# Row sums from the addition and squares on ScalarE at the feed-forward norms, with the next weights' first high parts emitted earlier

## The chip, the cores and the metric

The kernel runs on one core of a Trainium2 chip. Its time is the device time of one execution in microseconds, and each figure is a median over repeated runs on the same chip. A core has five engines that work side by side, each with its own queue, which it works off in order: TensorE (PE in the profile, with its weight loads as PEld) multiplies matrices, VectorE (DVE) and ScalarE (ACT) work on rows of 128 partitions, GpSimd (POOL) does a little setup, and SyncE (SP) issues most of the transfers from memory. Engines wait for each other by semaphores.

## The reference

Two layers over 256 tokens of width 1024, in float32. Each layer is a half-step feed-forward block, a mixer and another half-step feed-forward block, each followed by a layer norm over the residual:

```python
for l in range(DEPTH):
    h = _swiglu(x, ffn_w1[l, 0], ffn_w3[l, 0], ffn_w2[l, 0])
    x = _layernorm(ALPHA * x + 0.5 * h, ln_g[l, 0], ln_b[l, 0])
    h = _mixer(x, l, ...)
    x = _layernorm(ALPHA * x + h, ln_g[l, 1], ln_b[l, 1])
    h = _swiglu(x, ffn_w1[l, 1], ffn_w3[l, 1], ffn_w2[l, 1])
    x = _layernorm(ALPHA * x + 0.5 * h, ln_g[l, 2], ln_b[l, 2])

def _swiglu(x, w1, w3, w2):
    return (jax.nn.silu(x @ w1) * (x @ w3)) @ w2

def _layernorm(x, g, b):
    mu = jnp.mean(x, axis=-1, keepdims=True)
    var = jnp.mean(jnp.square(x - mu), axis=-1, keepdims=True)
    return (x - mu) * lax.rsqrt(var + LN_EPS) * g + b
```

The mixer (a gated spatial unit, differential attention, gates and an output projection) is not touched by the change.

## The kernel before

The 256 tokens are two tiles of 128 (`t` = 0, 1), the width is two halves of 512 (`c`, or `h`). Every weight comes from memory as a raw block of 128 x 2048 numbers (`raw_pool`, four buffers). `stream` (L154) loads it and splits it: ScalarE copies it to a reduced-precision high part (L173, `whi`), and VectorE subtracts that from the raw block for the low part (L177, `wlo`). A product is the sum of three: high by high, low by high, high by low (`three`, L217). The pools for high and low parts hold eight pieces each.

TensorE's order is written out by hand. The other engines' orders come from a planner at compile time: each instruction has a priority, its place in the program (`step` raises it by 1000 for every block), and goes into its engine's queue when the planner reckons its inputs ready, lower numbers first. `soon` lowers the number by two blocks; `behind(x)` orders an instruction behind x on the same engine. The queues are then worked off as they stand.

`ffn` (L569) ends with the products by the second weight. Four pairs of row blocks are held back (`HELD`): their weights are split early, all eight pieces of the pools, and their products come last, in the order tile 0 half 0, tile 0 half 1, tile 1 half 0, tile 1 half 1, each 24 products of one bank. After each bank the sum goes to the residual `x_tok` and to the norm:

- `Norm.part` (L485) adds the bank to the residual (L490) and takes VectorE's statistics of the 512 columns (bn_stats, L495). It is ordered behind the x split of tile 0, half 0, once there is one.
- `Norm.finish` (L499) joins the statistics (bn_aggr, L502), computes the inverse root on VectorE (`rsqrt`, L185: `ve`, a start value, three rounds of two operations, L189 to L195) and normalises both halves (L506); `ends[t]` is the last of these.
- `Norm.more` (L478) adds other contributions of tile 1 to the residual (L481, L483), behind `ends[0]`.
- `Norm.turned` and `turn` (L546) follow as a side task, at set places in TensorE's order: TensorE transposes a normalised half (L550), ScalarE applies gain and bias (L556, `xf`) and makes x's high part (L182), VectorE its low part (L183). `xlo[t, h]` is that last one.

The next layer begins with `gemm_b2` (L323), two sources of two blocks each. Its first block, and the first half of its second, are split into slots lent from the pool of activations (`lhi`, `llo`), because the pools are full of held pieces; the second half of the second block and the two later blocks go to the pools as the held products free them (`whi`, `wlo`, here 512 wide). Two ordering cells serve this: `early[0]` is the last lent high part, and later high parts go behind it; `after` puts low parts behind `ends[0]` (second and third block) or behind `xlo[0, 1]` (fourth). `gemm_b2` multiplies tile 0 with half 0 of x by blocks one and two (24 products), then half 1 by blocks three and four; tile 1's transposes come after 30 and 42 of these products.

There are three feed-forward norms with a layer behind them, two norms behind mixers, and the last norm, which ends the kernel (`last`) and has its own way through `finish`.

Of the kernel before, what the change touches and what calls it, by code (L numbers as in the profile page):

```python
# [20 lines left out]
P = 128  # L21
# [36 lines left out]
def trunk(ctx, tc, x, xT, w13a, w13b, w2s, w2p, wb, wqk, wa, wbr, wo, gateb, sgug, sgub, sguwT, sgubias, lam, diffg,  # L58
# [18 lines left out]
    def name(s):  # L77
        serial[0] += 1
        return f"{s}_{serial[0]}"
# [24 lines left out]
    def s512(s, n=4):  # L104
        return tmp.tile([P, 512], F32, tag="side", name=name(s), bufs=n)
# [6 lines left out]
    def step():  # L112
        chunk[0] += 1
        tc.cur_priority = chunk[0] * STEP

    tc.cur_priority = 0
    @contextmanager
    def soon():
        was = tc.cur_priority
        tc.cur_priority = max(0, was - 2 * STEP)  # L120
        yield
        tc.cur_priority = was
# [27 lines left out]
    def behind(ins):  # L150

        return tc.issue_after(ins) if ins is not None else nullcontext()

    def stream(src, width=CH, sub=HC, lent=(), after=(None, None)):  # L154

        step()
        raw = raw_pool.tile([P, CH], F32, tag="raw", name=name("raw"))
        nc.sync.dma_start(raw[:, :width], src)  # L160
        out = []
        for o in range(0, width, HC):
            if o // HC in lent:
                hi, lo = ([act.tile([P, 512], F32R, tag="slot", name=name(n)) for _ in range(2)] for n in ("lhi", "llo"))
                at = [(hi[j], lo[j]) for j in range(2)]
            else:
                hi = hi_pool.tile([P, HC], F32R, tag="hi", name=name("whi"))
                lo = lo_pool.tile([P, HC], F32R, tag="lo", name=name("wlo"))
                at = [(hi[:, p : p + sub], lo[:, p : p + sub]) for p in range(0, HC, sub)]
            for p, (h, w) in zip(range(0, HC, sub), at):  # L170
                r = raw[:, o + p : o + p + sub]
                with behind(latest[0] if o // HC in lent else early[0] or latest[0]):
                    copied = A.activation(h, r, AF.Copy)  # L173
                if o // HC in lent:
                    early[0] = copied.ins
                with behind(after[o // HC] or latest[1]):
                    V.tensor_tensor(out=w, in0=r, in1=h.bitcast(F32), op=ALU.subtract)  # L177
            out.append((hi, lo))
        return out

    def split(hi, lo, src):
        a = A.activation(hi, src, AF.Copy)  # L182
        return a.ins, V.tensor_tensor(out=lo, in0=src, in1=hi.bitcast(F32), op=ALU.subtract).ins  # L183

    def rsqrt(v, eps):  # L185


        ve, y = sm("ve", 1), sm("yi", 1, I32)
        V.tensor_scalar(out=ve, in0=v, scalar1=eps, scalar2=None, op0=ALU.add)  # L189
        V.tensor_scalar(out=y, in0=ve.bitcast(I32), scalar1=-0.5, scalar2=RSQRT_START, op0=ALU.mult, op1=ALU.add)  # L190
        y = y.bitcast(F32)
        for e in (-26 / 27, -8 / 9, -2 / 3):
            a, z = sm("nwa", 1), sm("nwy", 1)
            V.tensor_scalar(out=a, in0=y, scalar1=y, scalar2=ve, op0=ALU.mult, op1=ALU.mult)
            V.tensor_scalar(out=z, in0=a, scalar1=3.0 * 2.0 ** e, scalar2=y, op0=ALU.subtract, op1=ALU.mult)  # L195
            y = z
        return y
# [125 lines left out]
    def gemm_b2(srcs, xh, xl, done, norm=None):  # L323

        lent, after = [()] * 4, [(None, None)] * 4
        if norm:
            lent = [(0, 1), (0,), (), ()]
            after[1:3] = [(norm.ends[0], norm.ends[0])] * 2  # L330
        ps = [[bank() for _ in range(2)] for _ in range(NT)]
        got = [[None] * 4 for _ in range(2)]
        for t in range(NT):
            for c in range(2):
                if norm:
                    norm.ready(t, c)
                    after[3] = [norm.xlo.get((0, 1))] * 2
                for m in range(2):
                    n = 2 * c + m
                    if t == 0:  # L340
                        got[m][2 * c : 2 * c + 2] = stream(srcs[m][:, c * CH : (c + 1) * CH], sub=512, lent=lent[n],
                                                           after=after[n])
                    for i in range(2 * c, 2 * c + 2):
                        rows_b(ps[t][m], t, 2 * i, got[m][i], xh, xl, KT)
            early[0] = None
            with behind(latest[0] if t == 0 else None):
                done(t, ps[t])
# [104 lines left out]
    class Norm:  # L452
# [5 lines left out]

        def __init__(self, l, i, scale, eps, after, last=False):
            self.scale, self.eps, self.last, self.done = scale, eps, last, set()  # L460
            self.ends, self.xlo = [None] * NT, {}
            self.gT, self.bT = (v[:, l, i] for v in (ln_g, ln_b))
            self.y = x_tok
            self.group = 256 if last else 512
            self.st = [sm("st", D // self.group * 6, bufs=2) for _ in range(NT)]
            self.g, self.b = bc_load(lng[l, i], after), bc_load(lnb[l, i], after)
            if last:
                A.activation(self.g, self.g, AF.Copy, scale=-0.5)
                self.minus = s512("minus")
                A.activation(self.minus[:, :P], ident, AF.Copy, scale=-1.0)  # L470
                self.eps_t = self.minus[:, 2 * P : 2 * P + 1]
                V.memset(self.eps_t, eps)
                with behind(silu[0]):
                    A.activation(sm("first", 1), mask[:, :1], AF.Sqrt)
            else:
                self.x = [xs.tile([P, 4, 512], F32R, tag="x", name=name("x")) for _ in range(2)]

        def more(self, t, c, v, op, scale=1.0):  # L478
            y = self.y[t][:, c * 512 : (c + 1) * 512]
            if scale == 1.0:  # L480
                V.tensor_tensor(out=y, in0=y, in1=v, op=op)  # L481
            else:
                V.scalar_tensor_tensor(out=y, in0=y, scalar=scale, in1=v, op0=ALU.mult, op1=op)  # L483

        def part(self, t, c, ps, scale=None):  # L485
            s = slice(c, c + ps.shape[1])
# [59 lines left out]
        def turn(self, t, h):  # L546
            self.done.add((t, h))
            b = side_bank()
            for k in range(4):
                PE.transpose(b[:, k * P : (k + 1) * P], self.y[t][:, h * 512 + k * P : h * 512 + (k + 1) * P], ident)  # L550
            xf = s512("xf")
            hi, lo = (self.x[h][:, :, o + t * P : o + (t + 1) * P] for o in (0, T))
            with soon():
                for k in range(4):
                    s, f = slice(k * P, (k + 1) * P), slice(h * 4 + k, h * 4 + k + 1)
                    A.activation(xf[:, s], b[:, s], AF.Identity, scale=self.gT[:, f], bias=self.bT[:, f])  # L556
                with behind((None, self.ends[1])[h] if t == 0 else None):
                    last = split(hi, lo, xf.rearrange("p (k t) -> p k t", k=4))
            self.xlo[t, h] = last[1]
            if (t, h) == (1, 1):  # L560
                latest[:] = last
# [4 lines left out]
                x_cat = self.x  # L566
            return self

    def ffn(l, f, i, norm, last=False):  # L569
        xh, xl = parts(both)  # L570
        h_hi, h_lo = ({q: act.tile([P, 512], F32R, tag="slot", name=name(n)) for q in PQ} for n in ("hhi", "hlo"))
        p_hi, p_lo = h_hi, h_lo
# [100 lines left out]
        for m in range(HELD // 2):  # L673
            q = PQ[len(PQ) - HELD + 2 * m :][:2]
            held.update({(k, 1): w for k, w in zip(q, stream(w2p[l, f, len(PQ) - HELD // 2 + m]))})
        for t in range(NT):
            for c in range(2):
                for ps, o, n in ends[t, c]:
                    for q in PQ[-HELD:]:
                        rows_p(ps, t, q, held[q, c], hh, hl, o, n, stop=q == PQ[-1])  # L680
                    for o in ((0, 256) if last and (t, c) == (1, 1) else (0,)):
                        ln.part(t, c * 512 + o, ps[:, o : o + 256] if o or last and (t, c) == (1, 1) else ps, 1.0)
            ln.finish(t, ((2, 1.5), (2, 1))[t])
            if t == 0:
                with behind(ln.ends[0]):
                    ln.more(1, 0, S[7], ALU.subtract, ln.scale)
                    ln.more(1, 0, u, ALU.add)
                    ln.more(1, 1, v, ALU.add, ln.scale)
                    ln.more(1, 1, S[7], ALU.add)
# [223 lines left out]

    norm = None
    for l in range(DEPTH):
        norm = ffn(l, 0, 0, norm)
        norm = mixer(l, 1, norm)
        norm = ffn(l, 1, 2, norm, last=l == DEPTH - 1)


_INS = ["x", "xT", "w13a", "w13b", "w2s", "w2p", "wb", "wqk", "wa", "wbr", "wo", "gateb", "sgug", "sgub", "sguwT", "sgubias",
# [89 lines left out]
```

## Time and profile before

| what | us |
| --- | --- |
| median of 3 runs (1223.28 to 1223.63) | 1223.49 |
| the profiled execution | 1223.12 |
| its span, first to last instruction | 1221.4 |
| VectorE busy | 955.1 |
| ScalarE busy | 811.5 |

The page gives busy time by engine, shares of the span, and groups of instructions by source line; the trace behind it gives the order of time on each engine and what ended each idle stretch. A row of an order of time reads: start, duration, engine, line, operation, output <- inputs, shapes, count; in brackets the idle time before it and what ended it. An engine's next instruction can begin before the row of the one in front ends: a 128x512 operation of VectorE has a row of 0.68 us, and the next starts 0.60 us after it. The granted clock of TensorE was 0.999 in this execution.

### The profile page before, as it was taken

The page shows a single profiled execution, that of the slowest core. Times are in us where ns is not written, and L with a number is a line of the kernel's source. Part 1 is how long each engine was busy: PE and PEld are TensorE (multiplying, and loading weights), DVE is VectorE, ACT ScalarE, POOL GpSimd, SP SyncE. Part 2 cuts the span into 40 slices and gives each one's busy share as a digit, 9 for nine tenths or more (in the row PEclk, how much of TensorE's full clock was granted, in tenths as well). Part 3 has the DMA queues.
Part 4 walks back from the last instruction along what each step waited for, and adds up shares of the span by engine and source line. Part 5 has one row for each costly group of instructions (what it writes and reads, how often), then busy time and mean ns, then how long its engine had stood idle before and what let it go on. Part 6 is the DMA issues. An engine that isn't in the chain of part 4 may idle for free.

```text
span 1221.4 us, 16592 instructions
## 1 busy us (share of the span) xinstructions
PE 1210.1 (99%) x6033; PEld 1018.4 (83%) x6033; DVE 955.1 (78%) x1540; ACT 811.5 (66%) x1328; POOL 89.0 (7%) x184
## 2 busy tenths in 40 slices
PE   9999999999999999999999999999999999999998
PEld 8888887888888888888878888878888888888886
DVE  6658998886587985679985679979856879747797
ACT  7677657679665575776666776566795655667761
POOL 0100000244100000000000000003430000000000
PEclk9999999999999999999999999999999999999999
DMA  8975665654744657665667655666456446576551
GB/s 319 333 245 180 220 221 210 215 169 166 249 170 167 215 184 255 192 205 207 216 211 257 196 174 207 240 221 209 161 171 238 172 166 249 175 239 206 182 200 50
DMA packets 82339, 252.29 MB, mean 207 GB/s; under 512 B 47520, under 2 KB 48592, under 8 KB 55632
## 3 DMA queue, kind: packets, MB, share of 16 engines
q1 hardware_dynamic: 78288, 238.31, 57.5%
q0 software_dynamic: 3536, 12.13, 3.0%
q8 instruction: 47, 0.77, 0.3%
q10 hardware_dynamic: 432, 0.79, 0.2%
q14 instruction: 36, 0.29, 0.1%
HBM read 235.47 MB, written 1.05 MB: 194 GB/s over the span
## 4 chain that ended last, share of the span: by engine, by line
PE 82%; DVE 13%; issue 3%; ACT 2%; DMA 0%; DVEq 0%; ACTq 0%
PE bank L217 30%; PE sbank L217 17%; PE bank L229 17%; PE bank L236 9%; DVE wlo L177 3%; PE sbank L229 2%; DVE slo L301 2%; PE bank L389 2%; PE sbank L741 1%; DVE llo L177 1%; DVE raw L312 1%; ACT shi L299 1%; DVE xtok L490 1%; DVE st L495 1%; DVE raw L314 1%
## 5 line engine op out<-in xcount | busy, mean ns | idle before, releaser
L177 DVE TENSOR_TENSOR wlo<-raw,whi 128x1024 fp32r<-128x1024 f32 (+1 forms) x402 | 441.1, 1113 | 159.2 <-ACT whi L173 119.1
L173 ACT ACTIVATE whi<-raw 128x1024 fp32r<-128x1024 f32 (+1 forms) x402 | 378.2, 968 | 162.6 <-PE bank L217 61.7
L217 PE MATMUL bank<-whi,x 128*128 128x512 f32 x840 | 264.6, 390 | 0.0
L217 PEld LDWEIGHTS bank<-whi,x 128*128 128x128 f32 x840 | 157.7, 188 | 32.4
L217 PE MATMUL bank<-wlo,x 128*128 128x512 f32 x420 | 163.5, 389 | 0.0
L217 PE MATMUL sbank<-whi,x 128*128 128x512 f32 x512 | 158.9, 389 | 0.0
L229 PE MATMUL bank<-x,whi 128*128 128x512 f32 x640 | 158.3, 395 | 0.0
L229 PEld LDWEIGHTS bank<-x,whi 128*128 128x128 f32 x640 | 116.5, 188 | 25.9 <-issue 2.7
L217 PEld LDWEIGHTS sbank<-whi,x 128*128 128x128 f32 x512 | 96.1, 188 | 19.9
L299 ACT ACTIVATE shi<-raw 128x1024 fp32r<-128x1024 f32 (+1 forms) x80 | 73.4, 946 | 51.6 <-DVE raw L314 26.4
L217 PE MATMUL sbank<-wlo,x 128*128 128x512 f32 x256 | 99.6, 389 | 0.0
L301 DVE TENSOR_TENSOR slo<-raw,shi 128x1024 fp32r<-128x1024 f32 (+1 forms) x80 | 85.3, 1086 | 14.1 <-ACT shi L299 13.1
L217 PEld LDWEIGHTS bank<-wlo,x 128*128 128x128 f32 x420 | 78.9, 188 | 16.1
L236 PE MATMUL bank<-x,wlo 128*128 128x256 f32 x640 | 85.9, 285 | 0.0
L236 PEld LDWEIGHTS bank<-x,wlo 128*128 128x128 f32 x640 | 81.6, 191 | 2.3
L556 ACT ACTIVATE xf<-sbank,ln_b,ln_g 128x128 f32<-128x128 f32 x80 | 30.1, 458 | 63.2 <-PE sbank L550 63.2
L237 ACT ACTIVATE r<-bank 128x256 f32<-128x256 f32 x112 | 41.8, 379 | 27.6 <-PE bank L236 27.6
L217 PEld LDWEIGHTS sbank<-wlo,x 128*128 128x128 f32 x256 | 48.0, 188 | 10.1
L217 PE MATMUL sbank<-whi,hhi 128*128 128x512 f32 x144 | 56.4, 391 | 0.0
L217 PE MATMUL sbank<-wlo,hhi 128*128 128x512 f32 x144 | 56.1, 389 | 0.0
L217 PE MATMUL sbank<-whi,hlo 128*128 128x512 f32 x144 | 56.1, 389 | 0.0
L449 POOL DMA_DIRECT2D bc<-in_lng x6 | 3.2, 529 | 711.9 <-DVE bc L448 711.9
(233 smaller groups left out, 1976.9 us busy)
## 6 DMA issues: line engine op xcount, KB each, us to landing
raw<-in_w13b SPq DMA_DIRECT2D x76, 1024.0 KB, 5.2
raw<-in_w2p SPq DMA_DIRECT2D x24, 1024.0 KB, 4.9
raw<-in_wa SPq DMA_DIRECT2D x24, 1024.0 KB, 5.3
raw<-in_w2s SPq DMA_DIRECT2D x20, 1024.0 KB, 4.8
raw<-in_wb SPq DMA_DIRECT2D x16, 1024.0 KB, 5.3
raw<-in_wqk SPq DMA_DIRECT2D x16, 1024.0 KB, 4.9
raw<-in_wbr SPq DMA_DIRECT2D x16, 1024.0 KB, 4.8
raw<-in_w13a SPq DMA_DIRECT2D x8, 1024.0 KB, 4.8
```

What stands on the lines that cost most here:

```text
L173: copied = A.activation(h, r, AF.Copy)
L177: V.tensor_tensor(out=w, in0=r, in1=h.bitcast(F32), op=ALU.subtract)
L217: PE.matmul(ps, xx, w, start=start and n == 0, stop=stop and n == 2)
L229: PE.matmul(b[-1], hi[:, k * P : (k + 1) * P], xc(k), start=k == 0, stop=False)
L236: PE.matmul(b[n][:, :T], lo[:, k * P : (k + 1) * P], xc(k)[:, :T], start=False, stop=k == KT - 1)
L237: emptied[0] = A.activation(r[:, s], b[n][:, T:], AF.Copy, scale=scale).ins
L299: A.activation(h, r, AF.Copy)
L301: V.tensor_tensor(out=w, in0=r, in1=h.bitcast(F32), op=ALU.subtract)
L312: V.tensor_tensor(out=raw[:, :1024], in0=raw[:, :1024], in1=raw[:, 512:1536], op=ALU.add)
L314: last = V.tensor_tensor(out=raw[:, 1536:], in0=raw[:, 1024:1536], in1=raw[:, 1536:], op=ALU.add).ins
L389: PE.matmul(ps[t][m], x[:, j, o + t * P : o + (t + 1) * P], y, start=k0 + j == 0 and o == 0 and y is hi, stop=k0 + j == KT - 1 and y is lo)
L556: A.activation(xf[:, s], b[:, s], AF.Identity, scale=self.gT[:, f], bias=self.bT[:, f])
```

## The change

At the three feed-forward norms that have a layer behind them:

- `part_s` takes the place of `part`: one scalar_tensor_tensor adds the bank to the residual and puts the row sum of the result into a column of `st`. The bn_stats go, and the ordering behind the x split of tile 0.
- `finish_s` takes the place of `finish`: VectorE makes the negative mean from the two row sums, ScalarE squares the difference from the mean over the whole row of 1024 and sums it (the squares themselves go to a scratch tile in bf16 and are not read), `rsqrt` takes this sum with a scale of 1/D, and the normalisation adds the negative mean instead of subtracting the mean.
- `ahead` loads the next layer's first two blocks and emits their six lent high parts and the first four low parts in front of the held products. `rest_of` emits what is left of the two blocks in `gemm_b2`, where both were emitted whole before.
- `turn` orders tile 0's `xf` and x's high part behind the last lent high part.

`ffn` gets the first two blocks of the following layer (`following`) in place of the flag `last`.

```diff
+    def ahead(srcs):
+        pre = []
+        for m, n in enumerate((4, 2)):
+            step()
+            raw = raw_pool.tile([P, CH], F32, tag="raw", name=name("raw"))
+            nc.sync.dma_start(raw, srcs[m][:, :CH])
+            hi, lo = ([act.tile([P, 512], F32R, tag="slot", name=name(s)) for _ in range(n)] for s in ("lhi", "llo"))
+            for j in range(n):
+                with behind(early[0] or latest[0]):
+                    early[0] = A.activation(hi[j], raw[:, j * 512 : (j + 1) * 512], AF.Copy).ins
+            pre.append((raw, hi, lo))
+        lows(pre[0], latest[1])
+        return pre
+
+    def lows(p, after):
+        raw, hi, lo = p
+        for j in range(len(hi)):
+            with behind(after):
+                V.tensor_tensor(out=lo[j], in0=raw[:, j * 512 : (j + 1) * 512], in1=hi[j].bitcast(F32), op=ALU.subtract)
+
+    def rest_of(pre, after):
+        (_, hi0, lo0), (raw, hi1, lo1) = pre
+        lows(pre[1], after)
+        hi = hi_pool.tile([P, HC], F32R, tag="hi", name=name("whi"))
+        lo = lo_pool.tile([P, HC], F32R, tag="lo", name=name("wlo"))
+        for p in range(0, HC, 512):
+            r, h, w = (v[:, o + p : o + p + 512] for v, o in ((raw, HC), (hi, 0), (lo, 0)))
+            with behind(early[0]):
+                A.activation(h, r, AF.Copy)
+            with behind(after):
+                V.tensor_tensor(out=w, in0=r, in1=h.bitcast(F32), op=ALU.subtract)
+        return [(hi0[:2], lo0[:2]), (hi0[2:], lo0[2:])], [(hi1, lo1), (hi, lo)]
...
-    def rsqrt(v, eps):
+    def rsqrt(v, eps, scale=1.0):
...
+            V.tensor_scalar(out=ve, in0=v, scalar1=scale, scalar2=eps, op0=ALU.mult, op1=ALU.add)
...
-                    if t == 0:
+                    if t == 0 and n < 2 and norm and norm.pre:
+                        if n == 0:
+                            got[0][:2], got[1][:2] = rest_of(norm.pre, norm.ends[0])
+                    elif t == 0:
...
+        def part_s(self, t, c, ps):
+            y = self.y[t][:, c * 512 : (c + 1) * 512]
+            V.scalar_tensor_tensor(out=y, in0=y, scalar=1.0, in1=ps, op0=ALU.mult, op1=ALU.add,
+                                   accum_out=self.st[t][:, c : c + 1])
+
+        def finish_s(self, t, waits):
+            y, st = self.y[t], self.st[t]
+            minus, ss = sm("mv", 1), sm("ss", 1)
+            V.tensor_scalar(out=minus, in0=st[:, :1], scalar1=st[:, 1:2], scalar2=-1.0 / D, op0=ALU.add, op1=ALU.mult)
+            with soon():
+                A.activation(s512("sq").bitcast(BF16), y, AF.Square, bias=minus, accum_out=ss)
+            r = rsqrt(ss, self.eps, 1.0 / D)
+            for s in (slice(0, 512), slice(512, D)):
+                self.ends[t] = V.tensor_scalar(out=y[:, s], in0=y[:, s], scalar1=minus, scalar2=r,
+                                               op0=ALU.add, op1=ALU.mult).ins
+            beside(self.turned(t, waits), 0)
...
-            with soon():
+            with soon(), behind(early[0] if t == 0 else None):
...
+        if not last:
+            ln.pre = ahead(following)
         for t in range(NT):
             for c in range(2):
                 for ps, o, n in ends[t, c]:
                     for q in PQ[-HELD:]:
                         rows_p(ps, t, q, held[q, c], hh, hl, o, n, stop=q == PQ[-1])
+                    if not last:
+                        ln.part_s(t, c, ps)
+                        continue
...
-            ln.finish(t, ((2, 1.5), (2, 1))[t])
+            (ln.finish if last else ln.finish_s)(t, ((2, 1.5), (2, 1))[t])
...
+        norm = ffn(l, 0, 0, norm, [wb[l, 1, m] for m in range(2)])
+        norm = ffn(l, 1, 2, norm, [w13b[l + 1, 0, m, 0] for m in range(2)] if l < DEPTH - 1 else None)
```

More of the change, by code (lines that the diff above doesn't have):

```diff
@@ L183, in split @@
         return a.ins, V.tensor_tensor(out=lo, in0=src, in1=hi.bitcast(F32), op=ALU.subtract).ins
-    def rsqrt(v, eps):
+    def rsqrt(v, eps, scale=1.0):
         ve, y = sm("ve", 1), sm("yi", 1, I32)
-        V.tensor_scalar(out=ve, in0=v, scalar1=eps, scalar2=None, op0=ALU.add)
+        if scale == 1.0:
+            V.tensor_scalar(out=ve, in0=v, scalar1=eps, scalar2=None, op0=ALU.add)
+        else:
+            V.tensor_scalar(out=ve, in0=v, scalar1=scale, scalar2=eps, op0=ALU.mult, op1=ALU.add)
         V.tensor_scalar(out=y, in0=ve.bitcast(I32), scalar1=-0.5, scalar2=RSQRT_START, op0=ALU.mult, op1=ALU.add)
@@ L460, in __init__ @@
             self.scale, self.eps, self.last, self.done = scale, eps, last, set()
-            self.ends, self.xlo = [None] * NT, {}
+            self.ends, self.xlo, self.pre = [None] * NT, {}, None
             self.gT, self.bT = (v[:, l, i] for v in (ln_g, ln_b))
@@ L567, in close, with ffn @@
             return self
-    def ffn(l, f, i, norm, last=False):
+    def ffn(l, f, i, norm, following=None):
+        last = following is None
         xh, xl = parts(both)
@@ L915, in trunk @@
     for l in range(DEPTH):
-        norm = ffn(l, 0, 0, norm)
+        norm = ffn(l, 0, 0, norm, [wb[l, 1, m] for m in range(2)])
         norm = mixer(l, 1, norm)
-        norm = ffn(l, 1, 2, norm, last=l == DEPTH - 1)
+        norm = ffn(l, 1, 2, norm, [w13b[l + 1, 0, m, 0] for m in range(2)] if l < DEPTH - 1 else None)
 _INS = ["x", "xT", "w13a", "w13b", "w2s", "w2p", "wb", "wqk", "wa", "wbr", "wo", "gateb", "sgug", "sgub", "sguwT", "sgubias",
```

## The prediction

> **What bounds the kernel now.** I read the page first, then TensorE's waits, then each engine's order of time around the longest of them.
>
> ```profile
> span 1221.4 us, 16592 instructions
> PE 1210.1 (99%) x6033; PEld 1018.4 (83%) x6033; DVE 955.1 (78%) x1540; ACT 811.5 (66%) x1328; POOL 89.0 (7%) x184
> PE sbank L550 <- DVE xtok L506: 5.0, 3, 1.7
> ```
>
> TensorE is idle for 1221.4 - 1210.1 = 11.3 us in all. The first row of its waits (the last line: us in total, times, longest) puts 5.0 us of this into three waits of the transposes (L550) for the normalised rows (L506). Three feed-forward norms have a following layer, and the change touches just these. TensorE's order of time shows the three places:
>
> ```profile
> 189.28 0.39 PE L217 MATMUL bank<-whi,x 128*128 128x512 f32 x1
> 191.33 0.66 PE L550 MATMUL sbank<-ident,xtok 128*128 128x128 f32 x4 [1.65 <-DVE xtok L506]
> 616.78 0.66 PE L550 MATMUL sbank<-ident,xtok 128*128 128x128 f32 x4 [1.66 <-DVE xtok L506]
> 796.94 0.66 PE L550 MATMUL sbank<-ident,xtok 128*128 128x128 f32 x4 [1.66 <-DVE xtok L506]
> ```
>
> Three like gaps of 1.65 us, so one site stands for all. I take the first. The other norms (mixer, last) have no such wait on L506. VectorE's order of time there is the argument (start, us, line, operation):
>
> ```profile
> 171.45 0.68 DVE L490 TENSOR_TENSOR xtok<-xtok,sbank 128x512 f32<-128x512 f32 x1
> 172.16 0.69 DVE L495 BATCH_NORM_STATS2 st<-xtok 128x6 f32<-128x512 f32 x1
> 172.89 0.21 DVE L502 BATCH_NORM_AGGREGATE mv<-st 128x2 f32<-128x12 f32 x1
> 173.14 0.15 DVE L189 TENSOR_SCALAR ve<-mv 128x1 f32<-128x1 f32 x1
> ...
> 175.19 1.00 DVE L506 TENSOR_SCALAR xtok<-xtok,mv,nwy 128x512 f32<-128x512 f32 x2
> 176.11 0.68 DVE L483 SCALAR_TENSOR_TENSOR xtok<-xtok,sbank 128x512 f32<-128x512 f32 x1
> ...
> 178.51 0.68 DVE L490 TENSOR_TENSOR xtok<-xtok,sbank 128x512 f32<-128x512 f32 x1
> ...
> 179.71 0.68 DVE L495 BATCH_NORM_STATS2 st<-xtok 128x6 f32<-128x512 f32 x1
> ...
> 182.76 0.68 DVE L490 TENSOR_TENSOR xtok<-xtok,sbank 128x512 f32<-128x512 f32 x1
> ...
> 183.96 0.68 DVE L495 BATCH_NORM_STATS2 st<-xtok 128x6 f32<-128x512 f32 x1
> ...
> 185.15 0.20 DVE L502 BATCH_NORM_AGGREGATE mv<-st 128x2 f32<-128x12 f32 x1
> 185.27 0.63 DVE L177 TENSOR_TENSOR wlo<-raw,whi 128x512 fp32r<-128x512 f32 x1
> ...
> 187.95 0.20 DVE L195 TENSOR_SCALAR nwy<-nwa,yi 128x1 f32<-128x1 f32 x1
> 188.07 0.68 DVE L177 TENSOR_TENSOR wlo<-raw,whi 128x512 fp32r<-128x512 f32 x1
> ...
> 190.73 1.00 DVE L506 TENSOR_SCALAR xtok<-xtok,mv,nwy 128x512 f32<-128x512 f32 x2
> ```
>
> Token tile 0 is normalised alone, 1.69 us from its last addition (171.45) to `ve` (173.14). Tile 1's statistics chain is shared: after nearly every step of it stands one low part of the next weights (L177, one each 0.60 us). From the addition at 182.76 to the normalisation at 190.73 are 7.97 us, holding eight low parts and one x split (L183) besides the chain. VectorE hardly stops, as the windows of busy time say (columns: us, then busy us of PE, PEld, DVE, ACT, POOL, clock, DMA):
>
> ```profile
> 178.00:192.00 14.00, 12.35 (x60) 9.97 (x59) 13.65 (x30) 9.65 (x21) 0.00 (x0) 1.00 0.48 160
> ```
>
> VectorE is busy 13.65 of 14 us; so the gap's end is set by the amount of work ahead of L506 in its queue, and hardly by the length of the dependent chain. That decides how the change must be reckoned.
>
> **The change part by part.** *Row sums instead of statistics (`part_s`).* Four bn_stats per norm go, and a bn_aggr for each tile. The addition becomes a scalar_tensor_tensor with an accumulator output. The trace has none, but it has the plain form and another accumulating instruction:
>
> ```profile
> L483 DVE SCALAR_TENSOR_TENSOR xtok<-xtok,v x8: 679/681/683, 165.0 to 1201.5; 128x512 f32<-128x512 f32 x8
> L490 DVE TENSOR_TENSOR xtok<-xtok,sbank x13: 414/677/680, 171.5 to 1213.4; 128x512 f32<-128x512 f32 x11, 128x256 f32<-128x256 f32 x2
> 245.03 0.41 DVE L749 CUSTOM_DVE_ANT_0 pp<-sbank,mask 128x256 f32<-128x256 f32 x1
> 245.37 0.08 DVE L749 DVE_READ_ACCUMULATOR2_ANT mx<- 128x1 f32 x1
> 245.37 0.42 DVE L749 CUSTOM_DVE_ANT_0 pp<-sbank,mask 128x256 f32<-128x256 f32 x1
> ```
>
> 681 ns against 677: the form costs nothing. The accumulator read of 0.08 us lies beside the next instruction, which starts at the same 245.37. Bounds for the new addition: at the lower end nothing extra (two shapes of addition already differ by only 4 ns, so no gain is to be had there), above one more pass, 0.60. I take 0, as the nearest row (L749, also with one PSUM input and a sum) runs at the pace of a plain 256-wide operation. [...]
>
> *Squares on ScalarE (`finish_s`).* Per tile: one small VectorE operation `minus`, one Square over 128x1024 on ScalarE with accumulator output, then `rsqrt` as before (scale and eps in one instruction). ScalarE's groups by shape, and two rows of its order of time, price the Square:
>
> ```profile
> L173 ACT ACTIVATE whi<-raw 128x1024 fp32r<-128x1024 f32 x320 | 331.5, 1054 | 144.0 <-PE bank L217 53.3 <-PE bank L229 40.9 <-PE sbank L217 37.3
> L751 ACT ACTIVATE pp<-pp,mx 128x256 f32<-128x256 f32 x32 | 15.9, 498 | 12.9 <-DVE mx L749 12.9
> L751 ACT ACTIVATE pp<-pp,mx 128x128 f32<-128x128 f32 x32 | 12.4, 388 | 0.0
> L751 ACT ACTIVATION_READ_ACCUMULATOR pp<-pp,mx 128x1 f32 x64 | 12.0, 187 | 0.0
> ...
> 245.49 0.51 ACT L751 ACTIVATE pp<-pp,mx 128x256 f32<-128x256 f32 x1 [1.43 <-DVE mx L749]
> 245.91 0.18 ACT L751 ACTIVATION_READ_ACCUMULATOR pp<-pp,mx 128x1 f32 x1
> ```
>
> A copy of that size takes 1.05 us; from L751, which has a bias column and a sum, 498 + 768 x 110/128 = 1.16 us. The read ends 0.09 behind the end of its activation (246.09 against 246.00). I take 1.06 + 0.09 and 0.07 for two changes of engine, an estimate; upper end 0.11 more. What releases `ve` is then: tile 0, addition 0.72, read and `minus` 0.28 (bn_aggr takes 0.25), Square 1.22, so 2.22 against 1.69: **later by 0.53**. Nothing is ready to fill VectorE there, since the remaining low parts are ordered behind tile 0's normalisation (`after`, `ends[0]`). Its cover on TensorE: the first half is then ready at 175.19 + 0.50 + 0.53 = 176.22, and tile 0's transposes run at 177.65. So nothing is late there, but VectorE's queue behind it (from 176.11) starts 0.53 later.
>
> *Tile 1.* The shift of 0.53 is repaid by the bn_stats at 179.71 (0.60): the addition at 182.76 stands where it stood, and TensorE's own last product for it comes just ahead, so it cannot gain much. From there, 0.60 (bn_stats) and 0.12 (bn_aggr, 185.15 to 185.27) go; `minus` costs 0.12 to 0.15 (as L195 does, 187.95 to 188.07). The wait for the Square is covered by low parts: some 1.3 to 2 us against three of 0.60. Against that, `xf` of tile 0's second half stands on ScalarE just there:
>
> ```profile
> 167.90 0.63 ACT L173 ACTIVATE lhi<-raw 128x512 fp32r<-128x512 f32 x1 [0.48 <-DMA raw<-in_wb]
> 178.28 1.50 ACT L556 ACTIVATE xf<-sbank,ln_b,ln_g 128x128 f32<-128x128 f32 x4 [9.75 <-PE sbank L550]
> 179.67 0.64 ACT L173 ACTIVATE lhi<-raw 128x512 fp32r<-128x512 f32 x1
> ...
> 183.32 1.50 ACT L556 ACTIVATE xf<-sbank,ln_b,ln_g 128x128 f32<-128x128 f32 x4
> 185.22 0.64 ACT L182 ACTIVATE x<-xf 128x512 fp32r<-128x512 f32 x1
> 185.73 2.20 ACT L173 ACTIVATE whi<-raw 128x512 fp32r<-128x512 f32 x4
> ```
>
> The Square for tile 1 comes in at about 184.3 to 184.7, behind `xf`, and ends near 185.6. It delays x's high part (185.22) and the four `whi` by up to 1.1 us; the x split on VectorE then ends by about 187, and TensorE needs it after 24 products of 0.226 us from 182.58, at 188.0 (30 products lie from there to the gap, the last at 189.28). This fits by about 1 us. Then VectorE has still the x split and four low parts, 5 x 0.60 = 3.0 us, between the steps of `rsqrt`, as it does now. I allow 0.1 of idle time. Sum for one site: +0.53 - 0.60 - 0.60 - 0.12 + 0.15 + 0.1 = **-0.54; I say -0.6**, as the first `xf` and split come a little sooner (next part).
>
> *Early high parts (`ahead`, `rest_of`).* Six high parts (four of the first block, two of the second), four of their low parts and both DMAs are emitted ahead of the held products. Today five run by 168.5 and the sixth at 179.67, behind `xf`. That one moves into an idle stretch of 9.75 us; it frees 0.52 us at 179.67, and the `whi` behind it can use that stretch as well. The DMAs keep their place: SP issues nothing between the last `w2p` and these four, and each waits for its raw buffer as now. GpSimd's queue (the `bc` loads, issued earlier) is not passed. `xf` of tile 0 now waits for the sixth high part; behind it queue x's split and the transposed products. The cover is those 9.75 us. On VectorE the work is the same, so the gain is a tenth or so. The wait for `xlo` that `part` had is over by 181.6, before 182.76; dropping it gains nothing.
>
> Sum: 3 x -0.6 = **-1.8 us**. The profiled execution took 1223.12, 1.7 beyond its span; 1221.3 from there. The median shown is 1223.49, 0.37 higher, so I say **1221.7**. What is late next is still L506, with about 1.05 us of gap left at each site. Behind the gap TensorE's work is gapless, so what it gains there reaches the end.
>
> **Rivals.**
>
> *The gap closes.* If two of the five pieces on VectorE (x split, four low parts) come behind L506 instead of in front, 1.2 us more is gained and 1.65 is all there is. For it: the Square makes x's split later, and the last four low parts are ordered behind this split; the chain could run ahead of them. Against: one filler per step is the order today, and they are enough to fill every step. 3 x 1.65 = 5.0: **1218.5**.
>
> *The Square stands behind a blocked instruction (slower).* ScalarE's queue is in order. Tile 0's Square is ready at 172.45; the first `whi` of the second block is freed when TensorE has used a held block for the last time, six products (1.36 us) into tile 1, near 172.95. If the planner puts two such `whi` first, the Square starts at about 174.1, 1.65 later. Tile 0's first half comes at 177.9, past 177.65, and all of VectorE's queue follows: 190.1 + 1.65 = 191.75 for L506 against 190.73, so +1.0 at each site, **1226.5**. It decides from a wait of 0.6 us on. Against: the Square's priority is two steps ahead.
>
> *The accumulating addition runs at half pace.* Three additions per site count: 3 x 0.60 - 0.6 = +1.2, **1227.1**. [...]
>
> *Nothing moves.* The statistics were a filler in a full queue and the Square's wait eats their place: **1223.5**.
>
> **Numbers.** Part of the gap goes 0.44 (own range 1220.8 to 1222.6, 0.3 to 0.9 a site); it closes 0.22; the Square is blocked 0.13; half pace 0.07; nothing 0.14. A measurement can tell about 0.2%, 2.45 us. Faster by more: 0.22 and the forecast's lower edge 0.06, 0.28. Slower by more: 0.20. Between: 0.52. Range 1218.2 to 1227.0, from a closed gap to the half-pace bound.
>
> **What would show it.** Right: gaps of 0.8 to 1.3 us at L550 near 191, 616 and 797; tile 0's `ve` about 2.2 us behind its addition; fewer VectorE busy us by about 7 (12 bn_stats). Wrong: no gap and low parts behind L506 (closing), tile 0's Square starting over 0.6 us behind `minus` (blocked), additions of 1.2 us (half pace), or a new TensorE wait for `x` at 188.

## The result and the profile after

Times are in us; each ratio is between executions on one chip, with its 95% interval.

| | median | lowest to highest | executions | profiled execution | span |
| --- | --- | --- | --- | --- | --- |
| before | 1223.56 | 1223.26 to 1224.1 | 15 | 1223.12 | 1221.4 |
| after | 1221.16 | 1220.96 to 1222.14 | 15 | 1220.97 | 1219.3 |

The ratio is 0.9981 [0.9973, 0.9989]: 2.4 us gained, about 0.2% (1.3 to 3.3 us by the interval). The page of after opens with the span and the busy times:

```profile
span 1219.3 us, 16603 instructions
PE 1210.0 (99%) x6033; PEld 1018.2 (84%) x6033; DVE 948.8 (78%) x1540; ACT 820.0 (67%) x1340; POOL 87.7 (7%) x184
```

TensorE's waits open with the row that was 5.0 us before (us in total, times, longest):

```profile
PE sbank L608 <- DVE xtok L539: 2.9, 3, 1.0
```

TensorE is as busy as before (1210.0 against 1210.1), the span is 2.1 shorter, and the three waits for the normalised rows (now L608 for L539) fell from 5.0 to 2.9: that is the gain in the span. The medians lie 0.3 further apart, as before's profiled execution is 0.44 below its median and after's 0.19. The three gaps stand in TensorE's order of time:

```profile
189.28 0.39 PE L255 MATMUL bank<-whi,x 128*128 128x512 f32 x1
190.65 0.66 PE L608 MATMUL sbank<-ident,xtok 128*128 128x128 f32 x4 [0.98 <-DVE xtok L539]
615.41 0.65 PE L608 MATMUL sbank<-ident,xtok 128*128 128x128 f32 x4 [0.97 <-DVE xtok L539]
794.93 0.66 PE L608 MATMUL sbank<-ident,xtok 128*128 128x128 f32 x4 [0.97 <-DVE xtok L539]
```

The last product before the gap starts at 189.28 in both kernels, so absolute times can be compared here: the transposes come at 190.65 in place of 191.33. VectorE's order of time of after, around the first gap (start, duration, line, operation):

```profile
171.04 0.69 DVE L528 SCALAR_TENSOR_TENSOR xtok<-xtok,sbank 128x512 f32<-128x512 f32 x1
171.65 0.08 DVE L528 DVE_READ_ACCUMULATOR xtok<-xtok,sbank 128x1 f32 x1
171.77 0.21 DVE L534 TENSOR_SCALAR mv<-st 128x1 f32<-128x1 f32 x1
173.29 0.15 DVE L227 TENSOR_SCALAR ve<-ss 128x1 f32<-128x1 f32 x1 [1.31 <-ACT sq L536]
...
175.35 1.01 DVE L539 TENSOR_SCALAR xtok<-xtok,mv,nwy 128x512 f32<-128x512 f32 x2
...
182.89 0.68 DVE L528 SCALAR_TENSOR_TENSOR xtok<-xtok,sbank 128x512 f32<-128x512 f32 x1
183.49 0.09 DVE L528 DVE_READ_ACCUMULATOR xtok<-xtok,sbank 128x1 f32 x1
183.49 0.69 DVE L177 TENSOR_TENSOR wlo<-raw,whi 128x512 fp32r<-128x512 f32 x1
184.10 0.21 DVE L534 TENSOR_SCALAR mv<-st 128x1 f32<-128x1 f32 x1
184.22 1.29 DVE L177 TENSOR_TENSOR wlo<-raw,whi 128x512 fp32r<-128x512 f32 x2
185.62 0.15 DVE L227 TENSOR_SCALAR ve<-ss 128x1 f32<-128x1 f32 x1
185.81 0.15 DVE L228 TENSOR_SCALAR yi<-ve 128x1 int32<-128x1 int32 x1
186.00 0.27 DVE L232 TENSOR_SCALAR nwa<-yi,ve 128x1 f32<-128x1 f32 x1
...
190.04 1.00 DVE L539 TENSOR_SCALAR xtok<-xtok,mv,nwy 128x512 f32<-128x512 f32 x2
```

The normalisation of tile 1 starts at 190.04, 0.69 ahead of the 190.73 of before. The stretch from the last addition is 7.15 in place of 7.97, and it is still a nearly full queue. ScalarE's order shows the two Squares:

```profile
172.01 1.15 ACT L536 ACTIVATE sq<-xtok,mv 128x1024 bf16<-128x1024 f32 x1 [2.37 <-DVE mv L534]
173.07 0.19 ACT L536 ACTIVATION_READ_ACCUMULATOR sq<-xtok,mv 128x1 f32 x1
173.16 1.13 ACT L211 ACTIVATE whi<-raw 128x512 fp32r<-128x512 f32 x2
...
182.85 1.50 ACT L614 ACTIVATE xf<-sbank,ln_b,ln_g 128x128 f32<-128x128 f32 x4 [1.89 <-PE sbank L608]
184.34 1.15 ACT L536 ACTIVATE sq<-xtok,mv 128x1024 bf16<-128x1024 f32 x1
```

Tile 0's Square finds ScalarE idle and goes at once; the `whi` stands behind it, not in front. Tile 1's Square follows `xf` without a pause.

### The profile page after: what moved, and what is told of

The parts are those of the page before. It is cut to its first block, busy times and chain, and to the rows that moved or that the text cites. A ratio compares the mean times of both kernels' runs of the same rounds, so it can differ in the third digit from the quotient of the medians.

```text
span 1219.3 us, 16603 instructions
## 1 busy us (share of the span) xinstructions
PE 1210.0 (99%) x6033; PEld 1018.2 (84%) x6033; DVE 948.8 (78%) x1540; ACT 820.0 (67%) x1340; POOL 87.7 (7%) x184
## 3 DMA queue, kind: packets, MB, share of 16 engines
HBM read 235.47 MB, written 1.05 MB: 194 GB/s over the span
## 4 chain that ended last, share of the span: by engine, by line
PE 97%; DVE 1%; ACT 1%; DMA 0%; issue 0%; DVEq 0%; ACTq 0%
PE bank L255 36%; PE sbank L255 26%; PE bank L267 17%; PE bank L274 9%; PE sbank L267 2%; PE bank L430 2%; PE sbank L274 1%; PE sbank L805 1%; PE sbank L608 1%; DVE wlo L177 1%; PE sbank L854 1%; PE sbank L935 1%; ACT xf L614 0%; ACT sq L536 0%; PE sbank L852 0%; PE sbank L876 0%
```

## The experiments

The theory: TensorE waits at each site for tile 1's normalisation, and that comes when VectorE's queue has worked off all that stands ahead of it; what counts is the amount of work, not which step of the norm it belongs to. The rivals: the shorter dependent chain of the sums made the gain; or the early parts did; or the change removed a bound that nothing else could have removed.

Beside the times, each kernel's gap is told (TensorE's idle time at the three sites, by its waits). It is the better measure, as profiled executions reach the first gap up to 0.8 apart from each other (the last product starts at 189.28 in before and after, at 189.22 in `e3_after_late_lows`, at 190.00 in `e6_before_two_late_lows`) for reasons that lie further ahead.

### The sums without the early parts, the early parts without the sums

`e1_sums_only`, from after (`ahead` is not called, and both blocks are emitted whole in their old place):

```diff
-        if not last:
-            ln.pre = ahead(following)
```

> The changed kernel without the early high parts: row sums and Square stay, the next layer's blocks are emitted behind the norm as before. Theory A (the gap's end is set by the amount of VectorE work queued ahead of tile 1's normalisation; the statistics were part of that amount): the gap at the transposes stays at about 1.0 to 1.2 us a site, 1221.2 to 1221.7 us. Rival B (the early high parts, which fill ScalarE's idle stretch and bring x's split sooner, give the gain): the gap is back at 1.65, 1223.5 us.

`e2_early_only`, from after (the statistics are bn_stats and bn_aggr again):

```diff
-                    if not last:
-                        ln.part_s(t, c, ps)
-                        continue
...
-            (ln.finish if last else ln.finish_s)(t, ((2, 1.5), (2, 1))[t])
+            ln.finish(t, ((2, 1.5), (2, 1))[t])
```

> The kernel before with the early high parts alone: bn_stats and bn_aggr stay. Theory A: VectorE has the same work ahead of tile 1's normalisation, so the gap stays between 1.5 and 1.7 us, 1223.0 to 1223.5 us. Rival B: the gap falls to about 1.0, 1221.2 us.

Measured: `e1_sums_only` 1221.73 (1221.43 to 1222.15), before on that chip 1223.45, ratio 0.9987 [0.9977, 0.9996], gaps 3.3 in all. `e2_early_only` 1226.07 (1224.08 to 1227.33), ratio 1.0022 [1.0012, 1.0031], gaps 5.6. So the sums bring about 1.7 of the 2.4. The early parts take another 0.4 of gap away when the sums are there; this rests on the gaps alone, as the intervals of `e1_sums_only` and of after overlap. Alone they make the kernel slower, which I had not expected. VectorE's order in `e2_early_only` says why:

```profile
183.64 0.68 DVE L548 TENSOR_TENSOR xtok<-xtok,sbank 128x512 f32<-128x512 f32 x1
...
189.54 0.68 DVE L177 TENSOR_TENSOR wlo<-raw,whi 128x512 fp32r<-128x512 f32 x1
190.14 0.27 DVE L232 TENSOR_SCALAR nwa<-nwy,ve 128x1 f32<-128x1 f32 x1
190.44 0.21 DVE L233 TENSOR_SCALAR nwy<-nwa,nwy 128x1 f32<-128x1 f32 x1
190.69 0.27 DVE L232 TENSOR_SCALAR nwa<-nwy,ve 128x1 f32<-128x1 f32 x1
191.00 0.21 DVE L233 TENSOR_SCALAR nwy<-nwa,nwy 128x1 f32<-128x1 f32 x1
191.25 1.00 DVE L564 TENSOR_SCALAR xtok<-xtok,mv,nwy 128x512 f32<-128x512 f32 x2
```

Behind the last addition stand seven low parts and x's split, one low part fewer than in before; that one is done ahead of the addition. No work is saved: against TensorE's last product the addition is 0.56 later (183.64 to 189.60, in before 182.76 to 189.28). And at the end there is a filler fewer (an independent operation between two dependent steps), so that four steps of the inverse root stand bare, where before had two. A bare step there costs 0.25 to 0.31, one with an independent low part behind it 0.12 to 0.19 (in before 187.16 to 187.35, 187.95 to 188.07). So the gap is 1.87 in place of 1.65, 0.6 in all over three sites. The fastest execution is 1.1 slower than before's fastest (1224.08 against 1222.95), so 0.5 of that is not in these gaps. The median is 2.0 us above the fastest, and no gap accounts for it. The same kernel once more, to see whether this belongs to it:

> The early high parts alone once more, as its times lay between 1224.1 and 1227.3 us with granted clocks from 1.000 to 0.997. If that spread belongs to the kernel, the long runs with a clock of 0.997 to 0.998 come again here and not in the other kernels of this set; if it was the chip at that time, all its times lie near 1224.2 us, which is what its gaps of 1.87 us (5.6 in all against 5.0) make.

`e8_early_only_again`, without any edit to `e2_early_only`: 1226.69 (1225.64 to 1229.46), before 1223.44, ratio 1.0027 [1.0018, 1.0037], the same gaps. It belongs to the kernel; the last section has the cause of most of it.

### The queue reordered, with and without the change

If the amount of work ahead of the normalisation is what counts, low parts that nobody needs yet can go behind it. `after[3]` orders the fourth block's four low parts behind tile 0's last x split; they are put behind tile 1's normalisation, in after and in before:

```diff
-                    after[3] = [norm.xlo.get((0, 1))] * 2
+                    after[3] = [norm.ends[1] if norm.pre else norm.xlo.get((0, 1))] * 2
```

> The changed kernel with the four low parts of the fourth block ordered behind tile 1's normalisation instead of between the steps of its inverse root. Theory A: some 4 x 0.5 = 2 us less work ahead of it, against 0.98 us of gap left, so all three gaps close, 3 x 0.98 = 2.9 us less: 1218.2 us, and the low parts still come in time for their products (from about 191). Rival C (the gap that is left is the length of the dependent chain through ScalarE): the steps only wait for each other, the gap stays near 0.98, 1221.2 us. If the low parts come too late, TensorE waits for wlo instead, up to 1 us a site.

In before a flag `ffn`, set at the feed-forward norms, takes the place of `norm.pre`:

> The kernel before, with only that one reordering of four low parts, statistics and all. Theory A: about 2 us less ahead of the normalisation against a gap of 1.65, so the gap closes to 0 or 0.1: 3 x 1.6 = 4.9 us less, 1218.6 us, with none of the change in it. Rival C: 1223.5 us, as the chain is as long as before.

Measured: `e3_after_late_lows` 1217.94 (1217.57 to 1218.71), `e4_before_late_lows` 1218.01 (1217.62 to 1218.39), before 1223.45, and the ratio is 0.9956 [0.9941, 0.9971] for both. In neither do TensorE's waits have a row for the normalised rows any more. VectorE's order of `e3_after_late_lows`:

```profile
188.08 1.00 DVE L539 TENSOR_SCALAR xtok<-xtok,mv,nwy 128x512 f32<-128x512 f32 x2
189.00 2.49 DVE L177 TENSOR_TENSOR wlo<-raw,whi 128x512 fp32r<-128x512 f32 x4
```

And VectorE's order of `e4_before_late_lows`:

```profile
188.87 1.00 DVE L506 TENSOR_SCALAR xtok<-xtok,mv,nwy 128x512 f32<-128x512 f32 x2
189.78 2.49 DVE L177 TENSOR_TENSOR wlo<-raw,whi 128x512 fp32r<-128x512 f32 x4
```

With TensorE's order there, the last product and the transposes:

```profile
189.32 0.39 PE L217 MATMUL bank<-whi,x 128*128 128x512 f32 x1
189.55 0.60 PE L550 MATMUL sbank<-ident,xtok 128*128 128x128 f32 x4
```

The four low parts stand behind the normalisation, which in before now starts at 188.87 in place of 190.73, ahead of the transposes by more than its first half takes (0.50). The change still makes it earlier (188.08 against 188.87), but TensorE has no use for that: its own products fill the time up to 189.5. So one ordering cell gives 5.4 us, more than twice what the change gives, and with it the change gives nothing that can be measured. These two are the fastest kernels here.

The span of both fell by 5.5 (1221.4 to 1215.9) where the gaps held 5.0. Start to start says why: from the last product to the transposes 189.28 to 191.33 is 2.05 in before, and here 0.23, so a gap costs 1.82, 0.17 more than its idle row. The row counts the last product with 0.39, though the next one could start 0.23 after it. 3 x 1.82 = 5.5.

Half of it, `e6_before_two_late_lows` (two of the four behind, in before):

```diff
-                    after[3] = [norm.xlo.get((0, 1))] * 2
+                    after[3] = [norm.xlo.get((0, 1)), norm.ends[1] if norm.ffn else norm.xlo.get((0, 1))]
```

> The kernel before with only two of the four low parts of the fourth block ordered behind tile 1's normalisation. Theory A, by the amount of work: each low part takes 0.60 us, and a step of the inverse root that loses its filler costs some 0.12 more by itself, so 0.48 each: the gap falls from 1.65 to about 0.7, 3 x 0.96 = 2.9 us less, 1220.6 us. If one order or the other is all that counts (nothing or everything), 1223.5 or 1218.0 us.

Measured: 1220.6 (1220.37 to 1221.25), before 1223.44, ratio 0.9976 [0.9967, 0.9985]; TensorE's waits:

```profile
PE sbank L550 <- DVE xtok L506: 2.2, 3, 0.7
```

The gap is 2.8 less and the time 2.84 less.

### Work added

Three kernels add work ahead of the normalisation in before, at tile 1 only. `e7_before_extra_stats` takes the bn_stats of half 1 twice; `e9_before_one_small` and `e10_before_three_small` put one and three small operations of 128x1 at the head of `finish`, whose output nobody reads (in VectorE's queue they come right behind the bn_stats of half 0, at 180.48 in `e10_before_three_small`, ahead of the last addition):

```diff
+                for _ in range(2 if ffn and (t, c) == (1, 512) else 1):
...
+            for j in range(more):
+                V.tensor_scalar(out=sm("pad", 4)[:, j : j + 1], in0=self.st[t][:, :1], scalar1=1.0, scalar2=None, op0=ALU.add)
```

> The kernel before with one bn_stats more at tile 1's second half (the same statistics once again). Theory A: 0.60 to 0.75 us more work ahead of the normalisation, gaps of 2.25 to 2.4 us, 3 x 0.6 to 0.75 more: 1225.3 to 1225.7 us. Rival: the operation finds a hole, 1223.5 us.

> The kernel before with one small independent VectorE instruction (128x1) more in tile 1's finish at the three feed-forward norms. Theory (the gap follows the amount of VectorE work ahead of tile 1's normalisation): the gap grows from 1.65 us by 0.06 to 0.2 us to 1.71 to 1.85 at each site, and the time comes to 1223.7 to 1224.1 us. Rival (the gap is the length of the chain): the instruction is in nobody's chain, so the gap stays 1.65 us and the time 1223.45 us. Open beside it: with gaps of 1.87 us some executions lost 2 us more at a lower granted clock, with 1.66 us none did; if the length of the gap is what counts, it begins between the two, so either answer is possible here.

> The same with three such instructions. Theory: gap 1.85 to 2.1 us at each site, fastest runs at 1224.0 to 1224.8 us. If the length of the gap alone decides whether the clock falls behind it, some executions show a mean granted clock of 0.998 or less and a time 1.6 to 3.5 us above the fastest; if something else in the kernels with 1.87 us gaps did it, all runs agree within 0.8 us at 0.999 or more. Rival (chain length): 1.65 us and 1223.45 us.

Measured: `e7_before_extra_stats` 1227.4 (1226.27 to 1229.69), before 1223.44, ratio 1.0035 [1.0024, 1.0045], gap 2.5 at each site: 0.85 more for an instruction of 0.60, the rest being two more bare steps at the end. `e9_before_one_small` 1224.04 (1223.29 to 1226.25), before 1223.39, ratio 1.0006 [0.9996, 1.0015]; by its time alone it can't be told from before, but its gap is 1.81 at each site, 0.16 more for an operation of 0.15. `e10_before_three_small` 1225.86 (1224.55 to 1227.49), before 1223.39, ratio 1.0021 [1.0012, 1.0031], gap 2.00, 0.35 more for three that take 0.34 in a row. These small operations are in nobody's chain, and in `e4_before_late_lows` the gap went with the chain as long as before: the rival of the shorter chain falls.

### The Square doubled

`e5_square_twice_t0`, from after, makes tile 0's Square twice, so that `ve` comes later as it would behind a blocked queue:

```diff
-            with soon():
-                A.activation(s512("sq").bitcast(BF16), y, AF.Square, bias=minus, accum_out=ss)
+            sq = s512("sq").bitcast(BF16)
+            for _ in range(2 - t):
+                with soon():
+                    A.activation(sq, y, AF.Square, bias=minus, accum_out=ss)
```

> The changed kernel with the Square of tile 0 done twice (the same numbers again), which stands for a Square that has to wait 1.1 us in ScalarE's queue. Theory A (VectorE's queue stands still until the sum comes, and all that is behind it moves by as much): tile 0's ve comes 1.06 to 1.15 later, the gaps grow from 0.98 to about 2.1 us, 3 x 1.1 = 3.3 us more than the changed kernel: 1224.5 us, slower than before. Rival D (tile 0 is alone early and has slack up to its transposes at 177.64): little or nothing, 1221.2 us.

Measured: 1228.0 (1225.69 to 1228.53), before 1223.44, ratio 1.0032 [1.0021, 1.0043], gaps of 2.3, more than the 2.1 expected. ScalarE's order at tile 0:

```profile
172.71 1.15 ACT L538 ACTIVATE sq<-xtok,mv 128x1024 bf16<-128x1024 f32 x1 [3.01 <-DVE mv L534]
173.76 0.19 ACT L538 ACTIVATION_READ_ACCUMULATOR sq<-xtok,mv 128x1 f32 x1
173.85 0.62 ACT L211 ACTIVATE whi<-raw 128x512 fp32r<-128x512 f32 x1
174.37 1.13 ACT L538 ACTIVATE sq<-xtok,mv 128x1024 bf16<-128x1024 f32 x1
```

And VectorE's row of `ve`:

```profile
175.63 0.15 DVE L227 TENSOR_SCALAR ve<-ss 128x1 f32<-128x1 f32 x1 [2.96 <-ACT sq L538]
```

A `whi` slipped in between the Squares, so VectorE stood idle 2.96, 1.65 more than in after, and the gap grew by 1.33 at each site. Idle time that nothing fills at tile 0 comes out, for the most part, at tile 1. The fastest execution is 4.7 above after's fastest (1225.69 - 1220.96), 4.0 of it the gaps; most of the others are longer still, as told in the last section.

### All kernels by their gap

| kernel | gap at a site | median | lowest | before beside it |
| --- | --- | --- | --- | --- |
| `e4_before_late_lows` | none | 1218.01 | 1217.62 | 1223.45 |
| `e3_after_late_lows` | none | 1217.94 | 1217.57 | 1223.45 |
| `e6_before_two_late_lows` | 0.7 | 1220.6 | 1220.37 | 1223.44 |
| after | 0.98 | 1221.16 | 1220.96 | 1223.56 |
| `e1_sums_only` | 1.1 | 1221.73 | 1221.43 | 1223.45 |
| before | 1.65 | 1223.44 | 1222.97 | |
| `e9_before_one_small` | 1.81 | 1224.04 | 1223.29 | 1223.39 |
| `e2_early_only` | 1.87 | 1226.07 | 1224.08 | 1223.45 |
| `e10_before_three_small` | 2.00 | 1225.86 | 1224.55 | 1223.39 |
| `e5_square_twice_t0` | 2.3 | 1228.0 | 1225.69 | 1223.44 |
| `e7_before_extra_stats` | 2.5 | 1227.4 | 1226.27 | 1223.44 |

The lowest times lie within 0.8 of 1218.0 and three times the gap. The medians do so up to a gap of 1.81; beyond it they lie higher.

## Why the prediction was right, point by point

**What bounds it.** Right: the gap follows the amount of VectorE work ahead of the normalisation, whether this is taken out of the norm (the change), moved behind it (`e4_before_late_lows`, `e6_before_two_late_lows`) or added beside it (`e9_before_one_small`, `e10_before_three_small`). The amount alone does not give the gap to a tenth: `e2_early_only` has the work of before and 0.22 more gap, by its bare steps.

**The sum.** -0.54 a site was worked out and -0.6 said, -0.69 measured (190.73 to 190.04); 1.05 of gap was to be left, 0.98 is. The mechanism was right, but that the sum came so close is in part luck: several terms were off, one by 0.57 up, one by 0.60 and one by 0.37 down, and nearly made up for each other. The reason for going from -0.54 to -0.6 did not hold either: tile 0's first `xf` came at 178.44 in place of 178.28, and the x split behind it at 181.08 in place of 180.95.

- *Tile 0's chain* came as worked out: 2.25 from the addition (171.04) to `ve` (173.29) against a forecast of 2.22. The shift of +0.53 did not: the normalisation moved only from 175.19 to 175.35, +0.16. The prediction let the addition stand at 171.45; the bn_stats of half 0 (169.05 before), which stood in front of it, is gone too, a term that the prediction put at nothing, and the addition came at 171.04. I had repaid the shift only later, with the bn_stats of tile 1's half 0.
- That one (179.71 before) brought the second addition nothing: a low part moved into its place, five between tile 1's two additions in place of four, and the second addition stands at 182.89 against 182.76, +0.13 (forecast: unchanged); ahead of that addition 0.03 of the 0.60 came.
- So the stretch to the normalisation holds one low part fewer, seven in place of eight: -0.60 which I did not have. With bn_stats -0.60, bn_aggr -0.12, `minus` +0.12 and some 0.2 of idle time at `ve` (184.22 + 2 x 0.60 = 185.42 against 185.62; I had 0.1), 7.97 would become 6.97; it is 7.15. The rest is mostly bare steps: `ve` and the start value take 0.19 each (185.62, 185.81, 186.00) where before had a filler behind either and went on after 0.06 (185.83 to 185.89), while at the end one step stands bare (189.80 to 190.04) where before had two (190.18, 190.48, 190.73). A filler moved away uncovers a step; that term the prediction lacked, and its remark that the fillers of before are enough for every step misses those two.

**The Square** took 1.15 (1.06 taken, upper end 1.16), its read 0.19 with 0.10 of it behind the Square's end (0.09 in the row used). The 0.07 for two changes of engine, an estimate with no row beside it, was 0.03 each (171.98 to 172.01, 173.26 to 173.29). ScalarE's busy time rose by 8.5, VectorE's fell by 6.3 (about 7 said).

**The early parts**: "a tenth or so" was their gain beside the sums, and 0.13 a site is measured (3.3 to 2.9 over three sites). That they would cost 0.2 a site without the sums was not seen.

**The rivals.** *Half pace* is refuted by the rows above: from 182.89 to the next at 183.49, the new addition with its sum keeps the pace of 0.60, and its row is 0.68. This holds for this addition, which has one source in PSUM (`sbank`); no run here has one with both in SBUF. *The Square blocked* did not happen (172.01, 0.03 behind the end of `minus`), but its mechanism and price are real: 1.65 of wait was to shift the normalisation by as much, to 1.0 over before's; `e5_square_twice_t0` shows 1.33 for 1.65, to 0.66 over before's (2.31 against 1.65). *The gap closes* did not happen with the change; its sum, 1218.5, and its way, low parts behind the normalisation, are what `e3_after_late_lows` and `e4_before_late_lows` show, at 1217.9 and 1218.0. The prediction named the lever and reckoned it as an accident of the planner; it is a matter of one ordering cell.

## What to carry to other kernels

When an awaited instruction stands in a full in-order queue, list what stands ahead of it and move out what nobody needs yet before making its own chain cheaper; one reordering was worth more than twice the change here, and made the change worthless. Here a filler of 0.60 between two dependent small steps saved some 0.12 and held the awaited instruction back by the rest, so it paid only where its own result was due before the end of the chain. A gain on the awaited engine stops at the point where the waiting engine's own work ends, so work out that point first (here 189.5).

## What the hardware showed beside it

**Behind gaps of 1.87 us and more TensorE's granted clock was 0.50 for 3.41 us, in some executions.** The kernels with gaps of up to 1.81 (118 executions with a clock on record, before among them) all show a mean granted clock of 0.999 or 1.000. A mean of 0.999 alone does not tell: in before's profile it comes from a half clock in the last 1.29 us, behind TensorE's last product, in those of `e7_before_extra_stats` and `e8_early_only_again` from a stretch behind a gap; but in before the 19 executions at 0.999 took 1222.97 to 1223.69, no longer than those at 1.000. Of the 46 executions with gaps from 1.87 to 2.5, 24 show 0.996 to 0.998, and they are mostly the longer ones: of `e10_before_three_small`, four at 0.999 took 1224.55 to 1224.99, two at 0.998 took 1225.79 and 1225.93, four at 0.997 took 1227.35 to 1227.49. The windows of its profile (0.997; columns: us, TensorE's busy time and instructions, granted clock, DMA share, GB/s) around its three gaps:

```profile
616.44:619.85 3.41, 1.42 (x9) 1.00 0.92 327
619.85:623.26 3.41, 3.41 (x10) 0.50 0.62 257
...
189.77:193.18 3.41, 1.47 (x9) 1.00 1.04 368
193.18:196.59 3.41, 3.41 (x10) 0.50 0.46 192
...
797.35:800.76 3.41, 1.77 (x8) 1.00 0.74 252
800.76:804.17 3.41, 3.04 (x15) 1.00 0.93 360
```

Behind the first and the second gap the clock is at 0.50 for 3.41 us, which loses 1.7 each: 2 x 1.7 and 3 x 0.35 of gap make 4.45, and the span is 4.3 longer than before's. In the 3.41 ahead of these two stretches TensorE is busy for 1.42 and 1.47. Behind the third gap, as long as the others (2.0), the clock stays at 1.00. The profile of `e7_before_extra_stats`, with gaps of 2.5, reads the same at its first gap; at its second the clock stays at 1.00:

```profile
189.26:192.67 3.41, 0.91 (x5) 1.00 0.93 336
192.67:196.08 3.41, 3.41 (x11) 0.50 0.64 269
615.92:619.33 3.41, 1.88 (x9) 1.00 0.73 216
619.33:622.74 3.41, 2.45 (x13) 1.00 1.01 396
```

And that of `e8_early_only_again`, at its third gap of 1.87 and at its second:

```profile
795.42:798.83 3.41, 1.54 (x9) 1.00 0.96 334
798.83:802.24 3.41, 3.41 (x12) 0.50 0.64 267
614.52:617.93 3.41, 1.75 (x8) 1.00 1.00 312
617.93:621.34 3.41, 3.20 (x16) 1.00 0.79 303
```

In `e9_before_one_small` (gaps of 1.81) the clock stays at 1.00 behind all three; behind the first:

```profile
191.90:193.90 2.00, 2.00 (x11) 1.00 0.94 336
193.90:195.90 2.00, 2.00 (x12) 1.00 0.51 213
195.90:197.90 2.00, 2.00 (x11) 1.00 0.00 0
```

So the length of a gap alone does not decide: of the three like gaps in the profiled execution two are followed by such a stretch in `e10_before_three_small`, one in `e7_before_extra_stats` and one in `e8_early_only_again`. These runs do not show what decides. The stretches account for most of what the medians of `e2_early_only`, `e8_early_only_again`, `e10_before_three_small`, `e5_square_twice_t0` and `e7_before_extra_stats` lie above their gaps; 0.5 to 0.8 is there in the fastest executions of the table too, three of them at a clock of 1.000, and stays open. None of the 10 executions with gaps of 1.81 has a mean clock below 0.999, of the 20 with 1.87 (`e2_early_only` and `e8_early_only_again`) 11 have. So additions of 0.2 and more to before's gap of 1.65 cost more than their length (three times 0.35 of gap cost 2.5 in the median of `e10_before_three_small`).

One execution of `e9_before_one_small` (1226.25, at a clock of 1.000) and one of `e8_early_only_again` (1229.46, where another at the same 0.997 took 1226.89) fit none of this and are left open.
